# Gate weight sums and the split output weight of a Fourier layer formed during the attention layer and kept in DRAM

## The chip, the cores and the metric

The kernel runs on one core of one Trainium2 chip. A core has five engines that each work through a queue of their own: TensorE (PE) multiplies matrices, with weight loads (PEld) beside it; VectorE (DVE) and ScalarE (ACT) work on tiles; GpSimd (POOL) does both small vector work and DMA issues; SyncE (SP) issues DMAs. Engines wait for each other by semaphores. Data lies in DRAM, is loaded into SBUF by 16 DMA engines, and matmuls write to PSUM. The metric is the time of one execution in microseconds (us).

## The reference

Two layers work on a prompt of 2048 tokens and a sample of 512, each with 1024 channels, in float32: a banded attention with a gate, then Fourier mixing with a gate. A final norm follows.

```python
def attention_layer(x, g, w_in, w_out, sink, rel_bias):
    h = rmsnorm(x, g)
    z = h @ w_in
...
    o = banded_gqa_with_sink(q, k, v, rel_bias, sink)
    return x + (o * jax.nn.silu(gate)) @ w_out

def fourier_layer(x, g, w_gate, w_out):
    b, s, d = x.shape
    h = rmsnorm(x, g)
    hg = h.astype(jnp.float32).reshape(b, s, N_FGROUPS, FGROUP_CH)
    f = jnp.fft.fftn(hg, axes=(1, 3), norm="ortho").real
    f = f.reshape(b, s, d).astype(x.dtype)
    gate = h @ w_gate
    return x + (f * jax.nn.silu(gate)) @ w_out
```

`w_gate` and the Fourier layer's `w_out` (`w_fout` in the kernel) are 1024 x 1024.

## The kernel before

**Arithmetic.** A float32 value is held as two f32r tiles, a rounded high part and the remainder. `matmul3` (L81) makes one product out of three matmuls: high by high, high by low, low by high. So every weight has to be split before use: a cast makes the high part, a subtraction the low part.

**Attention phase** (`attention_phase`, from L116). The tokens go in five chunks of 512. In chunk 0 `load_w` (L87) loads each of 28 weights of 128 x 1024, casts it on ACT (L97), forms the remainder on POOL in four pieces of 128 x 256 (L102), and stores both parts to DRAM (`wsd`, 1 MB each); the later chunks load them from there. In each chunk a loop runs 64 steps, over 8 pairs of heads, four blocks of 128 queries and two heads, plus five steps in which the last ones drain. One step's `scores` is a pair of matmuls into the PSUM tile `spt` (L385), a DVE instruction that adds the bias and finds the extreme (L397, into `S`), an exponential on ACT (L401), a reciprocal (L404) and a scaling (L406) on DVE. Three steps later `transp` turns the scores on PE (L417) and splits them on ACT (L418) and DVE (L419) into `pts`; two steps after that `av` (L431) multiplies with the values; `out_evac` (L436 to L449) gates the result into the tiles `uT`, with two small instructions on POOL. Projections of the next heads, and at the end `out_proj` (L453), fill PE between the steps. SBUF tiles of the tag "x" (4 KB per partition: activations that are loaded and normed) come from a ring of four buffers, `S` from five, `spt` from two. A tile that takes a used buffer waits until the last reader of the old tile is done. The statistics of the next chunk run in the second half of a loop (i from 28 on), in tiles of tag "x".

**Seam and Fourier phase** (`fourier_phase`, from L561). Tiles come from two rings, `left` (24 buffers) and `right` (16). Token tiles are treated in ten pairs. The gate of a pair is a 2 x 2 block product done with seven products in place of eight (`gates`, L710): with w_gate cut into quarters B11, B12, B21, B22, the weights used are B11, T1 = B12 - B11, T2 = B22 - T1, B22, T3 = B22 - B12, N4 = B21 - B11 - T3, and B21, each in four row blocks of 128 x 512, each split. `build1` (L786) loads two pieces of w_gate (`w32g`), and makes the split parts of B11, T1, T2 and B22 in `left`, and those of B21, which POOL stores to `b21d`. `build2` (L801) loads the same pieces again (`w32h`) and makes T3 and N4 in `right`. The sums are DVE's, the casts ACT's (L586), the remainders DVE's or POOL's (L587). At the end of attention out_proj's last steps are interleaved with the four `build1` calls and with the norms of the first pair, whose `x1` loads go out on ACT's queue (L637); then the first pair's transposes (`turn`, L662), two `build2`, the transforms over channels (`z`), two `build2`, and the gates. In `gates` ACT copies each finished product out of PSUM (L746); in each pair B21 is loaded anew from `b21d` on SP's queue, two blocks ahead. After the last pair `load_res` (L590, called at L1007) loads w_fout in eight pieces of 512 KB and splits it on ACT (L600) and DVE (L601), before the output positions (`position`, `split_T` at L623, `finish`) use it as `wo`.

**Order.** Each engine executes its instructions in the order in which the program issues them. A DMA is issued from the queue of the engine named in the code, so SP, ACT and POOL can each hold DMAs back that stand behind a waiting instruction. In `inv_rms` a norm has one small POOL instruction (a power) between its sum and its scaling.

Of the kernel before, what the change touches and what calls it, by code (L numbers as in the profile page):

```python
# [31 lines left out]
LINE = 512  # L32
HALVES = ((1, 0), (1, 1), (0, 0), (0, 1))
# [5 lines left out]
def f32(ap):  # L39
    return ap.bitcast(F32)  # L40
# [3 lines left out]
def encoder(  # L44
# [25 lines left out]
    wsd = [dram.tile([P, 2, D], F32R, name=f"wsd{i}") for i in range(28)]  # L70

# [44 lines left out]
    def attention_phase():  # L116

        with ExitStack() as es:
# [365 lines left out]

            HB = [(b, j) for b in range(4) for j in range(2)]
# [7 lines left out]
            for c in range(len(CHUNKS)):  # L493
# [19 lines left out]
                for i in range(64 + LAG + AVLAG):  # L513
# [47 lines left out]
    def fourier_phase(tail):  # L561
        with ExitStack() as es:
# [26 lines left out]

            def load_res(w, name, stage):  # L590

                res, steps = [], []

                def load(half, k2):
                    w32 = stage(f"w32{name}{half}_{k2}")
                    SP.dma_start(w32, w[half, k2])
                    for kk in range(2):
                        t = left([P, 2, 512], F32R, f"wr{name}{half}_{k2}_{kk}")
                        src = w32[:, kk * 512 : kk * 512 + 512]
# [4 lines left out]
                for half in range(2):  # L604
                    for k2 in range(4):
                        steps.append(lambda half=half, k2=k2: load(half, k2))
                return res, steps
# [101 lines left out]

            def gates(pr, hooks):  # L710
# [5 lines left out]
                b21 = []  # L716

                def more():
                    if len(b21) < 4:
                        t = right([P, 2, 512], F32R, f"b21_{n}_{len(b21)}")  # L720
                        SP.dma_start(f32(t), f32(b21d[len(b21)]))
                        b21.append((t[:, 0], t[:, 1]))

                def x_step(k):
                    prod(X, A[0, 1], b21, (k,), True)
# [14 lines left out]
                more()  # L740
                more()
# [32 lines left out]
            b21d = [dram.tile([P, 2, 512], F32R, name=f"b21d{k}") for k in range(4)]  # L774
            wg = {w: [None] * 4 for w in ("B11", "T1", "T2", "B22", "T3", "N4")}

            def stage_w(w, k, name):

                rows = []
                for r in (k, k + 4):  # L780
                    t = left([P, 2, 512], F32, f"w32{name}{r}")
                    SP.dma_start(t, w[:, r // 2, :, (r % 2) * 512 : (r % 2) * 512 + 512].rearrange("h p c -> p h c"))
                    rows.append(t)
                return rows[0][:, 0], rows[0][:, 1], rows[1][:, 0], rows[1][:, 1]

            def build1(k):  # L786
                def w(name):
                    return left([P, 2, 512], F32R, f"w{name}_{k}")
# [390 lines left out]
```

## Time and profile before

| what | us |
|---|---|
| three timed runs | 1748.26, 1742.92, 1749.68 |
| median of them | 1748.26 |
| the profiled execution | 1746.94 |
| its span in the trace | 1745.2 |
| DVE busy in it | 1204.3 (69%) |
| ACT busy | 865.3 (50%) |
| POOL busy | 323.6 (19%) |
| chunk 1's 64 steps, first exponential to last | 286.5 to 431.5 |
| out_proj's last matmuls start | 1141.9 |

The span goes from the first to the last recorded instruction; 1.7 us of the execution lie around it. The mean granted clock of PE is 0.978. The trace shows for each instruction its start, its duration and, where its engine was idle, the event that ended the idle time. 342.6 MB are moved by DMA, at 196 GB/s in the mean.

### The profile page before, as it was taken

How to read it: one execution, taken by the hardware profiler on the slowest of the kernel's cores; microseconds unless marked ns; L12 is line 12 of the kernel's file. 1: busy time of each engine (PE TensorE's matmuls, PEld its weight loads, DVE VectorE, ACT ScalarE, POOL GpSimd, SP SyncE). 2: the span in 40 equal slices, each digit the busy share in tenths (PEclk: the TensorE clock that was granted, in tenths of full speed). 3: DMA queues.
4: the chain of work that ended last, by engine and by line, in shares of the span. 5: the costliest groups of instructions: out<-in, count | busy, mean ns of one | idle time of the engine just before them, and what ended most of it. 6: DMA issues, size and time to landing. Idle time of an engine off the chain costs nothing.

```text
span 1745.2 us, 25593 instructions
## 1 busy us (share of the span) xinstructions
PE 1663.0 (95%) x8980; PEld 1422.9 (82%) x8980; DVE 1204.3 (69%) x2826; ACT 865.3 (50%) x1966; POOL 323.6 (19%) x411
## 2 busy tenths in 40 slices
PE   9999899999999999899999999957999998999998
PEld 7877778888788888888888888846888886788886
DVE  5898655888448785288862888467667657888553
ACT  6677533675236663266641666335444545343221
POOL 2467630111301113011130111131000000111100
PEclk9999899999999999999999999978999999999999
DMA  8477775363663545744449443565565559763331
GB/s 304 170 284 300 263 289 194 132 213 136 220 236 134 184 152 184 265 139 166 161 151 325 139 139 128 190 238 193 187 223 187 195 175 336 283 223 118 139 106 49
DMA packets 95293, 342.59 MB, mean 196 GB/s; under 512 B 11019, under 2 KB 21259, under 8 KB 77244
## 3 DMA queue, kind: packets, MB, share of 16 engines
q1 hardware_dynamic: 87100, 298.74, 48.9%
q0 software_dynamic: 7632, 40.90, 6.0%
q8 instruction: 72, 1.18, 0.3%
q10 hardware_dynamic: 432, 1.31, 0.2%
q14 instruction: 57, 0.47, 0.1%
HBM read 267.47 MB, written 73.43 MB: 195 GB/s over the span
## 4 chain that ended last, share of the span: by engine, by line
PE 72%; DVE 12%; DMA 8%; issue 4%; ACT 3%; POOL 2%; SPq 1%; DVEq 0%; POOLq 0%; ACTq 0%
PE av L431 5%; PE spt L385 5%; PE pt L417 5%; PE qp L85 4%; PE qp L83 4%; PE qp L84 4%; PE gp L83 3%; PE gp L85 3%; PE gp L84 3%; PE op L83 3%; PE op L85 3%; PE op L84 3%; PE fo L85 3%; PE fo L83 3%; PE fo L84 3%
## 5 line engine op out<-in xcount | busy, mean ns | idle before, releaser
L401 ACT ACTIVATE S<-S 128x385 f32<-128x385 f32 (+1 forms) x320 | 191.1, 597 | 55.9 <-DVE S L397 54.9
L418 ACT CAST pts<-pt 128x384 fp32r<-128x384 f32 (+1 forms) x320 | 144.5, 454 | 116.2 <-PE pt L417 111.4
L419 DVE TENSOR_TENSOR pts<-pt,pts 128x384 fp32r<-128x384 f32 (+1 forms) x320 | 168.5, 526 | 42.7 <-ACT pts L418 40.1
L397 DVE CUSTOM_DVE_ANT_0 S<-spt,b 128x385 f32<-128x385 f32 (+1 forms) x320 | 168.8, 528 | 34.3 <-PE spt L385 29.5
L446 POOL TENSOR_TENSOR o<-o,s 128x256 f32<-128x256 f32 x75 | 55.3, 738 | 689.7 <-DVE o L442 678.2
L385 PE MATMUL spt<-kwin,qab 128*128 128x384 f32 (+1 forms) x640 | 159.1, 330 | 8.9 <-DVE S L397 8.9
L406 DVE TENSOR_SCALAR S<-S 128x384 f32<-128x384 f32 (+1 forms) x320 | 149.3, 467 | 9.1
L417 PE MATMUL pt<-ident,S 128*128 128x128 f32 x896 | 150.7, 274 | 1.0 <-DVE S L404 0.6
L385 PEld LDWEIGHTS spt<-kwin,qab 128*128 128x128 f32 x640 | 118.5, 189 | 38.0 <-DVE S L397 12.8
L83 PE MATMUL gp<-h,wg 128*128 128x512 f32 x320 | 137.7, 430 | 0.0
L83 PE MATMUL qp<-h,wq 128*128 128x512 f32 x320 | 137.1, 429 | 0.6 <-ACT wq L97 0.6
L431 PEld LDWEIGHTS av<-pts,v 128*128 128x128 f32 x896 | 126.6, 189 | 11.5 <-DVE pts L419 0.2
L431 PE MATMUL av<-pts,v 128*128 128x256 f32 x896 | 135.1, 284 | 0.0
L83 PE MATMUL op<-wo,uT 128*128 128x512 f32 x320 | 126.8, 399 | 2.9 <-DVE xr L476 2.9
L85 PE MATMUL fo<-wrf,tTu 128*128 128x512 f32 x320 | 126.2, 394 | 3.2 <-DVE tTu L623 3.2
L417 PEld LDWEIGHTS pt<-ident,S 128*128 128x128 f32 x896 | 114.0, 141 | 16.9 <-DVE pts L419 4.3
L83 PE MATMUL fo<-wrf,tTu 128*128 128x512 f32 x320 | 126.9, 396 | 0.0
L84 PE MATMUL op<-wo,uT 128*128 128x512 f32 x320 | 126.6, 396 | 0.0
L85 PE MATMUL qp<-h,wq 128*128 128x512 f32 x320 | 126.2, 394 | 0.1
L85 PE MATMUL gp<-h,wg 128*128 128x512 f32 x320 | 125.9, 393 | 0.0
L85 PE MATMUL op<-wo,uT 128*128 128x512 f32 x320 | 125.9, 395 | 0.0
L84 PE MATMUL fo<-wrf,tTu 128*128 128x512 f32 x320 | 125.8, 393 | 0.0
(322 smaller groups left out, 4052.8 us busy)
## 6 DMA issues: line engine op xcount, KB each, us to landing
wq<-wsd SPq DMA_DIRECT2D x32, 1024.0 KB, 4.9
wg<-wsd SPq DMA_DIRECT2D x32, 1024.0 KB, 6.6
wo<-wsd SPq DMA_DIRECT2D x32, 1024.0 KB, 4.9
b<-b21d SPq DMA_DIRECT2D x40, 512.0 KB, 5.1
x<-x1d SPq DMA_DIRECT2D x38, 512.0 KB, 4.4
b<-rowd SPq DMA_DIRECT2D x40, 384.0 KB, 4.2
xs<-in_x_dram SPq DMA_DIRECT2D x23, 512.0 KB, 7.3
xr<-in_x_dram SPq DMA_DIRECT2D x40, 256.0 KB, 5.1
```

Source lines behind the costliest of these rows:

```text
L83: PE.matmul(out, a[0], b[0], start=start, stop=False, skip_group_check=more)
L84: PE.matmul(out, a[0], b[1], start=False, stop=False, skip_group_check=more)
L85: PE.matmul(out, a[1], b[0], start=False, stop=stop, skip_group_check=more)
L385: PE.matmul(ps[:, 2 + k0 * P : 2 + k1 * P], q, kwin[g][:, part, b * P + k0 * P : b * P + k1 * P], start=part == 0, stop=part == 1,)
L397: DVE.tensor_tensor_reduce(out=s[:, e0:e1], in0=ps[:, 1 + e0 : 1 + e1], in1=st["bias"][:, j, 386 - e1 : 386 - e0][:, ::-1], scale=1.0, sca ...
L401: last_exp[0] = ACT.activation(s[:, e0:e1], s[:, e0:e1], AF.Exp, bias=mn, scale=-1.0, accum_out=den)
L406: DVE.tensor_scalar(s[:, ks], s[:, ks], den, None, ALU.mult)
L417: PE.transpose(ps[:, kb, :], s[:, 1 + kb * P : 1 + (kb + 1) * P], ident)
L418: ACT.copy(hi[:, k0:k1, j, :], ps[:, k0:k1, :])
L419: DVE.tensor_tensor(lo[:, k0:k1, j, :], ps[:, k0:k1, :], f32(hi[:, k0:k1, j, :]), ALU.subtract)
L431: PE.matmul(out, v, pt[:, kb].rearrange("p h q -> p (h q)"), start=kb == k0 and part == 0, stop=kb == k1 - 1 and part == 1,)
L446: eng.tensor_tensor(of, of, res["s"][:, cs], ALU.mult)
```

## The change

The sums and splits of w_gate, and the split of w_fout, are formed inside the loops of attention chunks 1, 2 and 3, one step of the list `EXTRA` per loop step i from 4 to 27, and stored to DRAM as pairs of f32r parts: `sumd` (28 tiles of 512 KB, B21 among them) and `foutd` (16 tiles). `keep` makes one of them in a tile of tag "x": the cast on ACT, the remainder on POOL in two pieces, the store from POOL's queue. The sums are POOL's in pieces too. In the Fourier phase the parts are loaded by POOL's queue: 16 tiles into `left` after the fifth step of out_proj's tail, 8 into `right` after the first pair's transposes, 16 of `wo` at the end. B21 is loaded by SP as before, but the list runs on over all pairs, so the blocks of the next pair are loaded while this one is computed. The first pair's norms are issued two steps earlier, in reversed order. w_gate is read once (8 loads on SP in the loops, 4.2 MB) instead of twice; 44 stores (23 MB) are added, and 40 loads on POOL's queue (21 MB) take the place of the 8 loads of w_fout and the 16 of w_gate in the Fourier phase.

```diff
+SUMS = ("B11", "T1", "T2", "B22", "T3", "N4", "B21")
...
+    evd = dram.tile([4, 2, P, D], F32, name="evd")
+    sumd = {w: [dram.tile([P, 2, 512], F32R, name=f"{w}d{k}") for k in range(4)] for w in SUMS}
+    foutd = [dram.tile([P, 2, 512], F32R, name=f"foutd{k}") for k in range(16)]
...
+            def pieces(out, a, b, op):
+
+                for i in range(2):
+                    cs = slice(i * 256, i * 256 + 256)
+                    POOL.tensor_tensor(out[:, cs], a[:, cs], b[:, cs], op)
+
+            def keep(dst, src):
+
+                t = ap.tile([P, 2, 512], F32R, tag="x", bufs=4, name="kept")
+                ACT.copy(t[:, 0], src)
+                pieces(t[:, 1], src, f32(t[:, 0]), ALU.subtract)
+                POOL.dma_start(f32(dst), f32(t))
+
+            def gate_sums(k):
+
+                q = {}
+
+                def load():
+                    for r, a, b in ((k, "B11", "B12"), (k + 4, "B21", "B22")):
+                        t = ap.tile([P, 2, 512], F32, tag="x", bufs=4, name=f"w32g{r}")
+                        src = w_gate[:, r // 2, :, (r % 2) * 512 : (r % 2) * 512 + 512]
+                        after(SP.dma_start(t, src.rearrange("h p c -> p h c")), last_exp[0])
+                        q[a], q[b] = t[:, 0], t[:, 1]
+
+                def kept(w, src):
+                    return lambda: keep(sumd[w][k], q[src])
+
+                def sums():
+                    pieces(q["B22"], q["B22"], q["B12"], ALU.subtract)
+                    pieces(q["B12"], q["B12"], q["B11"], ALU.subtract)
+
+                def more():
+                    pieces(q["B11"], q["B11"], q["B22"], ALU.add)
+                    pieces(q["B21"], q["B21"], q["B11"], ALU.subtract)
+
+                return [load, kept("B11", "B11"), kept("B22", "B22"), kept("B21", "B21"), sums, kept("T3", "B22"),
+                        kept("T1", "B12"), more, kept("T2", "B11"), kept("N4", "B21")]
+
+            def fout_parts(half, k2):
+                st = []
+
+                def load():
+                    st.append(ap.tile([P, 2, 512], F32, tag="x", bufs=4, name=f"w32f{half}_{k2}"))
+                    after(SP.dma_start(st[0].rearrange("p k c -> p (k c)"), w_fout[half, k2]), last_exp[0])
+
+                return [load] + [lambda kk=kk: keep(foutd[half * 8 + k2 * 2 + kk], st[0][:, kk]) for kk in range(2)]
+
+            EXTRA = {1: [gate_sums(0), gate_sums(1)], 2: [gate_sums(2), gate_sums(3)],
+                     3: [fout_parts(h, k2) for h in range(2) for k2 in range(4)]}
...
+                    if i == 3:
+                        extra = [s for steps in EXTRA.get(c, []) for s in steps]
+                    if 4 <= i < 28 and extra:
+                        extra.pop(0)()
...
-            def load_res(w, name, stage):
...
-                        ACT.copy(t[:, 0], src)
-                        DVE.tensor_tensor(t[:, 1], src, f32(t[:, 0]), ALU.subtract)
-                        res.append((t[:, 0], t[:, 1]))
...
+            b21 = []
+
+            def more():
+
+                k = len(b21)
+                if k < 4 * len(pairs):
+                    t = right([P, 2, 512], F32R, f"b21_{k}")
+                    SP.dma_start(f32(t), f32(sumd["B21"][k % 4]))
+                    b21.append((t[:, 0], t[:, 1]))
+
...
-                b21 = []
...
-                    prod(X, A[0, 1], b21, (k,), True)
+                    prod(X, A[0, 1], b21[4 * n : 4 * n + 4], (k,), True)
...
-            b21d = [dram.tile([P, 2, 512], F32R, name=f"b21d{k}") for k in range(4)]
...
-            def stage_w(w, k, name):
...
-            def build1(k):
...
-                b11, b12, b21, b22 = stage_w(w_gate, k, "g")
-                wg["B11"][k] = split(w("B11"), b11)
-                DVE.tensor_tensor(b12, b12, b11, ALU.subtract)
-                wg["T1"][k] = split(w("T1"), b12)
-                DVE.tensor_tensor(b11, b22, b12, ALU.subtract)
-                wg["T2"][k] = split(w("T2"), b11)
-                wg["B22"][k] = split(w("B22"), b22, POOL)
-                t = w("B21")
-                split(t, b21, POOL)
-                POOL.dma_start(f32(b21d[k]), f32(t))
...
-            def build2(k):
...
-                b11, b12, b21, b22 = stage_w(w_gate, k, "h")
-                DVE.tensor_tensor(b22, b22, b12, ALU.subtract)
-                DVE.tensor_tensor(b21, b21, b11, ALU.subtract)
-                DVE.tensor_tensor(b21, b21, b22, ALU.subtract)
-                wg["T3"][k] = split(w("T3"), b22)
-                wg["N4"][k] = split(w("N4"), b21, POOL)
+            def load_sums(place, *names):
+                for w in names:
+                    for k in range(4):
+                        t = place([P, 2, 512], F32R, f"w{w}_{k}")
+                        POOL.dma_start(f32(t), f32(sumd[w][k]))
+                        wg[w][k] = (t[:, 0], t[:, 1])
...
-            builds = [lambda k=k: build1(k) for k in range(4)]
             for i, s in enumerate(tail):
                 s()
-                if i in (4, 6):
-                    pairs[0].norms((i - 4) // 2, ACT)
-                if i % 2 and builds:
-                    builds.pop(0)()
+                if i in (2, 4):
+                    pairs[0].norms((4 - i) // 2, ACT)
+                if i == 5:
+                    load_sums(left, "B11", "T1", "T2", "B22")
...
-            build2(0)
-            build2(1)
+            load_sums(right, "T3", "N4")
+            more()
+            more()
             for i, hf in HALVES:
                 pr.z(i, hf)
-            build2(2)
-            build2(3)
...
-            wo, loads = load_res(w_fout, "f", x_tile)
-            for s in loads:
-                s()
+            wo = []
+            for k in range(16):
+                t = left([P, 2, 512], F32R, f"wo{k}")
+                POOL.dma_start(f32(t), f32(foutd[k]))
+                wo.append((t[:, 0], t[:, 1]))
```

More of the change, by code (lines that the diff above doesn't have):

```diff
@@ L588, in split @@
                 return t[:, 0], t[:, 1]
-            def load_res(w, name, stage):
[L592 to L599, printed above, removed]
-                        ACT.copy(t[:, 0], src)
-                        DVE.tensor_tensor(t[:, 1], src, f32(t[:, 0]), ALU.subtract)
-                        res.append((t[:, 0], t[:, 1]))
[L604 to L607, printed above, removed]
             def split_T(src, name, flip=False):
@@ L715, in gates @@
                 X = bank(f"X{n}")
-                b21 = []
[L718 to L722, printed above, removed]
                 def x_step(k):
-                    prod(X, A[0, 1], b21, (k,), True)
+                    prod(X, A[0, 1], b21[4 * n : 4 * n + 4], (k,), True)
                     more()
@@ L738, in hook @@
                         h()
-                more()
-                more()
                 four = range(4)
@@ L872, in combine @@
                     SP.dma_start(gsd[i] if gi == 0 else evd[gi - 1, i] if i < 2 else odd[gi - 1, i - 2], r[i])
-            evd = dram.tile([4, 2, P, D], F32, name="evd")
             pr = pairs[0]
```

10 lines of the change are left out of this document (removed).

## The prediction, made before the change was run

> **What bounds the kernel now.** The page's busy shares and slices come first, to find where TensorE (PE) isn't the bound.
>
> ```profile
> PE 1663.0 (95%) x8980; PEld 1422.9 (82%) x8980; DVE 1204.3 (69%) x2826; ACT 865.3 (50%) x1966; POOL 323.6 (19%) x411
> PE   9999899999999999899999999957999998999998
> POOL 2467630111301113011130111131000000111100
> PEclk9999899999999999999999999978999999999999
> ```
>
> PE works 95% of the span, so a gain can only lie where it rests: slices 26 and 27, about 1134 to 1222 us, the seam between the phases. POOL is nearly empty after chunk 0, the room that the change uses. Next the waits of PE (total, times, longest), and the seam's timeline (start, duration, operation, wait and releaser).
>
> ```profile
> PE trb L662 <- DVE x L639: 16.4, 2, 16.1
> PE W L83 <- ACT c L746: 16.3, 1, 16.3
> PE spt L385 <- DVE S L397: 8.9, 6, 2.8
> PE X L83 <- DMA b<-b21d: 5.7, 6, 2.2
> PE fo L85 <- DVE tTu L623: 3.2, 1, 3.2
> ...
> 1158.45 1.97 PE L662 MATMUL trb<-ident,x 128*128 128x128 f32 x8 [16.13 <-DVE x L639]
> ...
> 1190.50 0.79 PE L83 MATMUL W<-wT,S 128*128 128x512 f32 x1 [16.28 <-ACT c L746]
> ```
>
> The two longest waits are one cause. The first transpose waits for a norm whose x1 load stands on ACT's queue behind casts that wait for w_gate; the second waits for a copy (L746) that stands on ACT behind casts of the second read of w_gate. Last, the windows: start and end, length, busy us and count of PE, PEld, DVE, ACT, POOL, granted clock, DMA share, GB/s.
>
> ```profile
> 160.00:230.00 70.00, 60.51 (x293) 49.19 (x292) 52.02 (x121) 37.02 (x84) 46.49 (x64) 0.90 0.76 265
> 300.00:360.00 60.00, 60.00 (x347) 52.55 (x346) 51.60 (x162) 40.42 (x103) 8.87 (x12) 1.00 0.42 141
> 1100.00:1150.00 50.00, 42.32 (x204) 34.70 (x202) 21.22 (x43) 14.30 (x31) 10.72 (x12) 0.96 0.69 249
> 1150.00:1180.00 30.00, 15.34 (x88) 13.37 (x88) 21.32 (x33) 12.88 (x23) 8.82 (x8) 0.73 0.55 188
> 1180.00:1200.00 20.00, 9.19 (x42) 7.51 (x42) 15.26 (x21) 12.33 (x24) 5.34 (x6) 0.66 0.69 244
> ...
> 1460.00:1470.00 10.00, 5.31 (x24) 4.14 (x25) 10.00 (x16) 6.20 (x12) 0.53 (x1) 0.83 0.88 319
> ```
>
> At the seam PE is half idle and its granted clock falls to 0.73 and 0.66. In chunk 1 (300 to 360) PE is full while DVE is already at 51.6 of 60; in chunk 0, where POOL splits weights (46.5 of 70), PE loses. The change moves chunk 0's kind of work into chunks 1 to 3.
>
> **Part 1, the seam: a gain.** Out_proj's last matmuls start at 1142, and the first pair's gates end at about 1211: 69 us. The work between, at full clock: four turns 4.0 us, 96 matmuls of 128x256 at their pitch of 0.12 us (11.5), 84 of 128x512 at 0.227 (19.1), together 34.6. So 34.4 us are lost: the two waits, the rest through the low clock. Removed are 16 loads of w_gate, 28 casts at 0.615, the DVE differences and splits, and four b21d stores. With no cast ahead of them the two x1 loads go out when ACT has made the last uT, 1120, and both norms are done by about 1130, ahead of out_proj's end: the first wait goes whole.
>
> What is late next are the 24 loads of sums, all on POOL's queue, in the order B11, T1, T2, B22, then T3, N4 once out_proj's weight buffers are free (1133 to 1142). Behind the first two stands the norm's small POOL instruction (pow), which waits for x1, so the stream runs from about 1130. At the 319 GB/s that 1460 to 1470 shows, four loads (2.1 MB) take 6.6 us, with SP's other reads about 7.5: T1 is in at 1138, T2 1145, B22 1153, T3 1160, N4 1168. PE wants them at about 1156, 1159, 1162, 1164 and 1177. Behind the last of them on POOL stand the pows of the second pair's norms; N4's last issue, eight loads ahead of its landing, comes at about 1155, and that pair's transposes are wanted at 1166, so they hide, with 11 us of cover. I leave 4 us (2 to 12) for the ramp: -30 (-22 to -33).
>
> **Part 2, B21.** Its reads now run ahead across pairs, where each pair began anew with two: of 5.7 us of X waits I take -3 (0 to -6).
>
> **Part 3, fout.** Eight SP loads, 16 ACT casts at 0.618 and 16 DVE subtractions at 0.684 become 16 POOL loads; that takes at most the 3.2 us wait and the slow clock around it. But bytes double, 4.2 to 8.4 MB, where the queue is full (1460 to 1480 moves 319 to 374 GB/s at shares of 0.88 and 1.02): 4.2 MB at 350 GB/s is 12 us of DMA time. The sample's table loads stand behind them on POOL. +2 (-8 to +8).
>
> **Part 4, attention: the loss.** Added are 44 keeps (28 for the gate, 16 for fout), each a cast on ACT, two pieces on POOL, and a 512 KB store that POOL issues, and 32 pieces for the sums. The rows of the same instructions (count: min/median/max):
>
> ```profile
> L102 POOL TENSOR_TENSOR wg<-w32g,wg x28: 712/737/783, 36.9 to 163.7; 128x256 fp32r<-128x256 f32 x28
> ...
> L586 ACT CAST wB<-w32g x12: 601/615/623, 1129.4 to 1161.3; 128x512 fp32r<-128x512 f32 x12
> ...
> L799 POOL DMA_DIRECT2D b21d<-wB x4: 571/582/597, 1136.2 to 1164.7; - x4
> ...
> DMA to landing us min/median/max: 4.3/5.2/7.2
> ```
>
> POOL gets 120 x 0.737 + 44 x 0.58 = 114 us, and ACT 44 x 0.615 = 27 us, over three chunks of some 150 us loops: room in the mean. The wait is the price. The "x" ring has four buffers, two held by the weights read, so the kept tile n needs the store of n-2 landed, and ACT, which runs in order, stands at that cast with all later exponentials (L401) and pts copies (L418) behind it; PE waits for those. One keep costs 0.615 + 1.474 + 0.58 = 2.67 us plus the landing L, and two run at a time: 13 x (2.67 + L) / 2 from first to last keep of a chunk. That is 45, 51 and 64 us for L = 4.3, 5.2 and 7.2. ACT's order allots 17 exponentials in chunk 1 and 16 in chunk 2 between these; at 2.30 us a step (64 from 286.5 to 431.5) 39 and 37 us. A tile is used some 4 us after it is ready (L397 of one step ends at 320.85, its bank is wanted again at 324.56), which absorbs 4. At L = 5.2: 51 - 39 - 4 = 8 in chunk 1, 10 in chunk 2, 1 in chunk 3, where three buffers serve the stores: +19. At 4.3 it is 6, at 7.2 about 48; the b21d row was measured in windows of 188 to 249 GB/s, the loop moves 141 plus what is added, so I take its median.
>
> Two queues more are passed. On SP the 16 loads (16 x 512 KB) wait for a ring buffer, and behind them stand the projections' weights (wq, wg); I count nothing, as the "w" ring holds four, about half a group of eight steps, 9 us; without that cover SP adds up to the same lag again, which is C's size. On POOL, out_evac's two small instructions wait behind the pieces; their product uT is wanted only by out_proj at the loop's end, so that hides too.
>
> DVE's scale (L406) also suffers beside POOL: 0.405 us mean in 300 to 360, 0.606 in 100 to 160, 0.852 in 160 to 230. A step has 2.30 x 8.4 / 60 = 0.32 us of DVE to spare, so +0.2 hides; +0.45 would cost 0.13 x some 60 steps, 8 us, at the same steps that the store wait delays, so I don't add it. [...]
>
> **Sum.** The profiled run took 1746.94 (span 1745.2, 1.7 around it): 1746.9 - 30 - 3 + 2 + 19 = 1735; the median of the three runs is 1.3 above it, so 1736.
>
> **Rivals.**
> A, the forecast: 1736, by itself 1726 to 1748. For it: waits of 16 us with a named cause; a ring too short by arithmetic.
> B, the stores keep pace: L near 4.3, as the loop's DMA share of 0.42 suggests; attention costs 6: 1723. Against it: chunk 0, where no ring of two holds ACT, lost 8.9 in spt waits alone. [...]
> C, the other side: landing grows as POOL, reads of the loop and stores meet. L = 7.2 costs 48: 1736 + 29 = 1765, slower. It decides from where the attention cost passes 31 us (L about 6.1). For it: wsd<-wg stores of 1 MB land in 9.2 us in chunk 0; against: that stretch moves 298 GB/s, the loop half.
> D, POOL's stream is late at the seam: at the 249 GB/s of 1100 to 1150, 20 loads and 5 MB of SP's reads, 15.5 MB, take 62 us from 1130, N4 in at 1192 against 1177: 15 lost, gain 15: 1751, no change. For it: one queue, with pow in front; against: 319 to 374 GB/s seen later.
>
> **How the numbers follow.** Chances: A 0.47, B 0.18, C 0.23, D 0.12. A measurement of this kernel tells about 0.5%, 8.7 us, from no change: faster is under 1739.5, slower over 1757. A is faster in 0.36 and the same in 0.11; B faster 0.18; C slower 0.21, same 0.02; D same 0.09, slower 0.03. So 0.54, 0.22, 0.24. The range goes from 1714 (B with the seam's -33 and B21's -6) to C's 1766. A's own range stands above.
>
> **What would show it.** Right: the trb and W waits gone, clock 0.95 or more from 1140 to 1200; spt, pt and av waits of about 19 us in chunks 1 and 2 while i is 4 to 28, behind an ACT that waits for kept stores; L406 at 0.5 to 0.6 there. Wrong: a seam still over 50 us; a W or Z wait for DMA (D); waits in the loops over 40 us (C) or under 8 (B); fo waits over 10 us at 1440 to 1480.

## The result, and the profile after

Over twelve runs each the changed kernel takes 1753.14 us (1748.47 to 1757.76), the kernel before 1748.12; the ratio is 1.0033, with an interval of 1.0021 to 1.0046. The change costs about a third of a per cent, where the forecast had a gain of 12 us. The profiled run took 1751.27 us, 4.3 more than the one before (1746.94).

First the busy slices and the waits of PE in the profile after (total us, times, longest).

```profile
PE   9999899899989899999999999998999998999998
POOL 2467732721305511305313011121000001112000
PEclk9999999899999999999999999998999999999999
```

```profile
PE spt L389 <- DVE S L401: 31.5, 20, 3.5
PE As L87 <- ACT gs L931: 7.7, 1, 7.7
PE z L87 <- DVE xr L480: 7.6, 1, 7.6
```

The hole of slices 26 and 27 (counted from 0) is gone, with both waits of 16 us. In its place PE has lost a tenth in slices 7 and 13, in the loops of chunks 1 and 2, with POOL at 7 and at 5 there; slice 11, where POOL is at 0, is the gap between these loops. The spt waits went from 8.9 to 31.5 us. The windows show the two sides, chunk 1's loop and the seam (columns as before).

```profile
300.00:360.00 60.00, 50.60 (x264) 42.65 (x264) 46.12 (x113) 33.66 (x85) 41.35 (x61) 0.91 0.67 229
...
1183.00:1225.00 42.00, 34.39 (x193) 30.57 (x192) 21.98 (x35) 19.30 (x36) 6.22 (x12) 0.88 0.89 349
```

From 300 to 360, where PE was full, it now works 50.6 of 60 us and its granted clock is 0.91; DVE and ACT do less there than before (46.1 against 51.6, 33.7 against 40.4), so neither of them is the bound: they stand. Over the steps 4 to 28 of the three loops:

```profile
293.08:365.42 72.34, 62.94 (x334) 53.38 (x334) 56.85 (x147) 41.64 (x105) 46.59 (x68) 0.93 0.67 237
535.19:608.13 72.94, 63.91 (x338) 53.24 (x337) 61.65 (x148) 42.56 (x106) 46.66 (x68) 0.95 0.63 228
780.59:848.33 67.74, 62.32 (x349) 52.42 (x348) 52.44 (x148) 43.65 (x109) 38.68 (x57) 1.00 0.81 287
```

Before, the same steps took 55.5, 57.5 and 57.5 us, with PE busy throughout. They now take 42.5 us more: PE stands idle in 23.9 of these, and the other 18.6 lie in matmuls that take longer.

Where the time went is read by setting the same events of the two traces beside each other: the last exponential of attention, out_proj's last matmul, the last matmul of the first and of the tenth pair's last gate product (W from N4), and the last matmul of the output (fo).

| stretch, us | before | after | difference | forecast |
|---|---|---|---|---|
| start to attention's last exponential | 1104.2 | 1144.9 | +40.7 | +19 |
| to out_proj's last matmul | 37.8 | 37.8 | 0 | 0 |
| the seam, to the first pair's last gate matmul | 68.7 | 42.0 | -26.7 | -30 |
| to the last pair's last gate matmul | 242.5 | 246.9 | +4.4 | -3 (B21) and, with the next row, |
| to the last output matmul | 283.9 | 270.1 | -13.8 | +2 (fout) |

The sum of the differences is 4.6 us. The last two stretches exchange some 30 matmuls at their border (1372 in the last one before, 1339 after), so their sum, -9.4 against a forecast of -1, says more than each of them. By chunk, the first exponentials of chunks 2, 3 and 4 come 17.6, 30.7 and 40.7 us later. Nearly all of it falls on the steps up to i = 24: in chunk 1 the shift is +3.7 at step 8, +8.6 at 16, +16.8 at 24, and then stands.

### The profile page after: what moved, and what is told of

It reads as the page before. It is cut to its first block, busy times and chain, and to the rows that moved or that the text cites. A ratio compares the mean times of both kernels' runs of the same rounds, so it can differ in the third digit from the quotient of the medians.

```text
span 1749.5 us, 25848 instructions
## 1 busy us (share of the span) xinstructions
PE 1667.1 (95%) x8980; PEld 1422.5 (81%) x8980; DVE 1190.6 (68%) x2774; ACT 857.7 (49%) x1966; POOL 440.9 (25%) x599
## 5 line engine op out<-in xcount | busy, mean ns | idle before, releaser
L389 PE MATMUL spt<-kwin,qab 128*128 128x384 f32 (+1 forms) x640 | 162.5, 336 | 31.7 <-DVE S L401 31.5
L410 DVE TENSOR_SCALAR S<-S 128x384 f32<-128x384 f32 (+1 forms) x320 | 174.1, 544 | 8.9
L450 POOL TENSOR_TENSOR o<-o,s 128x256 f32<-128x256 f32 x75 | 55.2, 736 | 416.1 <-DVE o L446 409.7
L87 PE MATMUL gp<-h,wg 128*128 128x512 f32 x320 | 139.2, 435 | 0.0
L87 PE MATMUL qp<-h,wq 128*128 128x512 f32 x320 | 137.3, 429 | 0.6 <-ACT wq L101 0.6
L89 PE MATMUL gp<-h,wg 128*128 128x512 f32 x320 | 127.1, 397 | 0.0
L87 PE MATMUL fo<-wo,tTu 128*128 128x512 f32 x320 | 125.9, 393 | 1.2 <-DVE x L973 1.2
L88 PE MATMUL gp<-h,wg 128*128 128x512 f32 x320 | 126.8, 396 | 0.0
L89 PE MATMUL qp<-h,wq 128*128 128x512 f32 x320 | 126.2, 394 | 0.1
L88 PE MATMUL qp<-h,wq 128*128 128x512 f32 x320 | 125.6, 393 | 0.0
```

The source lines that it names most:

```text
L87: PE.matmul(out, a[0], b[0], start=start, stop=False, skip_group_check=more)
L88: PE.matmul(out, a[0], b[1], start=False, stop=False, skip_group_check=more)
L89: PE.matmul(out, a[1], b[0], start=False, stop=stop, skip_group_check=more)
L389: PE.matmul(ps[:, 2 + k0 * P : 2 + k1 * P], q, kwin[g][:, part, b * P + k0 * P : b * P + k1 * P], start=part == 0, stop=part == 1,)
L410: DVE.tensor_scalar(s[:, ks], s[:, ks], den, None, ALU.mult)
L450: eng.tensor_tensor(of, of, res["s"][:, cs], ALU.mult)
```

## The experiments

In what follows "attention's end" is the shift of the last exponential against the kernel before, from the traces; a ratio is of times to the kernel before, with its interval. Of the names in the expectations, "lock" is the rival that POOL's instructions hold DVE: in the kernel before the scale (L406) took up to 3.421 us in 50 to 231, where POOL is busy for 111.2 of 181 us, and up to 0.839 in 231 to 1110, where it is busy for 136.0 of 879. "Work" is the rival that what was added to ACT and POOL is in the way as such.

### What holds the loops: stores, ACT, POOL alone

**No stores.** One line of `keep` is left out, and the Fourier phase loads other DRAM of the same size.

```diff
-                POOL.dma_start(f32(dst), f32(t))
```

> The changed kernel without the 44 stores of kept tiles; the Fourier phase loads as many bytes from wsd in their place, so its weights are not those of the reference. In the changed kernel's trace the last exponential of attention lies 40.8 us later than before (1144.9 against 1104.2). Theory (ring): ACT stands at the cast of a kept tile until a store two tiles back has landed; without stores nothing of that is left, and attention's end moves by 3 to 12 us in place of 41; time 1715 to 1727. [...]

Measured: 1743.79 us, ratio 0.9989 (0.9975 to 1.0003); attention's end +28.7. Without stores 12 of the 41 us go, and 28.7 stay: the theory of the forecast, that the ring alone holds ACT, falls. By chunk, the loops lose 13.4, 12.9 and 2.0 us in place of 16.6, 14.0 and 10.0. The waits that the theory is about do stand in the changed kernel, for instance in 285 to 365 (waits of ACT, all that name a kept tile's store or POOL):

```profile
ACT kept L498 <- DMA B11d<-kept: 6.9, 2, 4.7
ACT uT L452 <- POOL o L450: 6.0, 5, 1.6
ACT kept L498 <- DMA B22d<-kept: 2.3, 1, 2.3
ACT kept L498 <- DMA B21d<-kept: 2.3, 2, 1.9
ACT kept L498 <- POOL kept L493: 1.7, 1, 1.7
```

ACT's waits for POOL at uT were 4.5 us in this window before, so in the changed kernel the stores are the longer hold there. Without stores the waits for POOL take their place:

```profile
ACT uT L452 <- POOL o L450: 10.4, 6, 4.2
ACT kept L498 <- POOL kept L493: 4.8, 2, 3.5
ACT kept L498 <- POOL w32g L493: 3.8, 3, 1.6
```

In chunk 1 of this run no scale of DVE took over 0.9 us, so the scale's holds, which come up below, have no part in its 13.4 us.

In chunk 3 of the changed kernel the hold has one more link: the loads of w_fout, on SP's queue, wait for a store to free their buffer, and ACT waits for the loads (waits of SP in 770 to 850, of ACT in 780 to 850):

```profile
SPq L532 <- DMA foutd<-kept: 21.1, 4, 10.3
ACT kept L498 <- DMA w32f<-in_w_fout_dram: 10.0, 4, 3.7
```

**Casts on POOL.**

```diff
-                ACT.copy(t[:, 0], src)
+                for i in range(2):
+                    cs = slice(i * 256, i * 256 + 256)
+                    POOL.tensor_copy(t[:, 0, cs], src[:, cs])
```

> The changed kernel with the cast of a kept tile made by POOL in two pieces of 128x256 in place of ACT: ring, stores and POOL's other work stay, but the wait for a store now holds POOL, not ACT. Theory (ring): exponentials are free again, attention's end moves by 5 to 15 us in place of 41; time 1717 to 1730. Rival (lock): POOL does more, not less, so DVE is held more: attention's end moves by 41 to 55; time 1753 to 1768. Rival (ACT's work): 27 us of casts are gone from ACT: 15 to 25 in place of 41; time 1730 to 1738, and no store wait seen in the chain.

Measured: 1754.68 us, 1.0049 (1.0033 to 1.0065); attention's end +43.6. ACT has no kept cast left, and yet it stands, now at another place (waits of ACT, 285 to 365):

```profile
ACT uT L452 <- POOL o L450: 20.2, 5, 9.4
```

Out_evac multiplies on POOL (L450), and ACT casts the product into uT (L452). With POOL's queue full of pieces that product comes late, and ACT, in order, waits with all later exponentials behind it: 20.2 us in five times, against 4.5 in six before.

**POOL's pieces alone, in pairs.** Two pieces per step on a scratch tile, in the kernel before.

```diff
+                    if 1 <= c < 4 and 4 <= i < (26 if c < 3 else 20):
+                        for _ in range(2):
+                            after(POOL.tensor_tensor(scr, scr, scr, ALU.mult), last_exp[0])
```

> The kernel before with 120 pieces of 128x256 on POOL added in the loops of chunks 1 to 3 (two per step, on a scratch tile, nothing waits for them): no casts, no stores, no loads, the seam as before. Theory (ring): such work alone costs little, attention's end moves by 0 to 6 us; time 1748 to 1755. Rival (lock): most of the 41 us appear here: attention's end moves by 25 or more; time 1773 to 1790.

Measured: 1754.24 us, 1.0037 (1.0014 to 1.0061); attention's end +6.8.

**The same in runs of eight**, at two places in the four-step rhythm of out_evac (the diff shows the first; the second has `i % 4 == 3`).

```diff
+                    if 1 <= c < 4 and i % 4 == 1 and 4 <= i < (28 if c < 3 else 20):
+                        for _ in range(4 if i > 24 else 8):
+                            after(POOL.tensor_tensor(scr, scr, scr, ALU.mult), last_exp[0])
```

> The kernel before with the same 120 pieces on POOL as in the run with pieces alone, but in runs of eight in a row (5.9 us) in each fourth loop step, at i mod 4 = 1, where out_evac's own two POOL instructions have just been issued and the next come three steps (6.9 us) later. In pairs they moved attention's end by 6.8 us. Theory (backlog: POOL's queue holds ACT at the cast of uT and of kept tiles): nothing of out_evac stands behind a run, so 5 to 12 us; time 1749 to 1757. Rival (lock for a whole run): DVE's scale (L406) is held up to 5.9 us by each of 16 runs, 2 or more beyond the slack: 25 to 45; time 1772 to 1790.

> The same runs of eight, one step ahead of out_evac (i mod 4 = 3), so that its product on POOL (L446) stands behind a run, and ACT's cast of uT (L448) waits for it with all later exponentials behind it. Theory (backlog): ACT is held 2 to 5 us by each of 16 runs; attention's end moves by 15 to 40 us more than with the runs at i mod 4 = 1, and the waits of ACT's L448 for POOL are 30 us or more longer than before. Rival (lock): the place of a run does not matter, the same time as there within 5 us.

Measured: 1753.10 us, 1.0032 (1.0015 to 1.0049) and 1757.20 us, 1.0056 (1.0035 to 1.0078); attention's end +7.3 and +10.8.

**Runs with two inputs, and built as in `keep`.** The first reads two halves of another tile; the second subtracts an f32r part from float32 into f32r, and only the first piece of a run is ordered. The diff is that of the second, against the runs of eight.

```diff
-                            after(POOL.tensor_tensor(scr, scr, scr, ALU.mult), last_exp[0])
+                            ins = POOL.tensor_tensor(w3[:, 1, cs], w2[:, cs], f32(w3[:, 0, cs]), ALU.subtract)
+                            if j == 0:
+                                after(ins, last_exp[0])
```

> As the runs of eight at i mod 4 = 1, but each piece reads two different halves of a tile of tag x and writes a third place, as the pieces of keep do (the earlier ones read and wrote one place only, and DVE's scale was never held longer than 0.9 us by them; in the changed kernel L410 was held up to 3.65 us, until POOL's run of pieces ended). Theory (lock for a whole run, when POOL reads two places): L406 is held 3 us or more, often, and attention's end moves by 15 to 40 us; time 1762 to 1787. Rival (no such lock; L410's long times are something else): as before, 6 to 9 us; time 1751 to 1757.

> Runs of eight pieces at i mod 4 = 1 as before, but built as in keep: float32 minus the high part, f32r out, two halves in turn, and only the first piece of a run ordered behind an exponential, so that the others are ready at once. Theory (POOL's runs hold DVE when each next piece stands ready): L406 held 2 us or more several times a chunk, attention's end moves by 12 to 35 us; time 1758 to 1782. Rival (what holds DVE in the changed kernel is not the pieces as such): max under 1 us as in the other runs, 4 to 9 us; time 1750 to 1757.

Measured: 1752.23 us, 1.0041 (1.0023 to 1.0058), attention's end +5.6; and 1747.90 us, 1.0010 (0.9997 to 1.0024), +0.6. In all five DVE's scale took at most 1.0 us in chunks 1 to 3. But the traces limit what they say. `after` orders instructions where the program is built and makes nothing wait on the chip, so part of the pieces ran ahead of the loop (of chunk 1's 44 pieces 12 in pairs, 30 in the last), and a run came behind out_evac's instructions at both places: the waits of ACT for POOL at uT were 7.2 us in both, in 285 to 365. What is shown is that POOL's work that holds nobody up costs 1 to 11 us; a backlog ahead of out_evac, which one of them was to make, was not made by it.

### Two holds side by side

**ACT free of POOL.** To the casts on POOL comes uT's, in chunks 1 to 3.

```diff
-                    ACT.copy(uT[:, 0, cs], of)
+                    if eng is POOL and c in (1, 2, 3):
+                        POOL.tensor_copy(uT[:, 0, cs], of)
+                    else:
+                        ACT.copy(uT[:, 0, cs], of)
```

> The changed kernel with the cast of kept tiles on POOL, and in chunks 1 to 3 also out_evac's cast of uT on POOL: ACT has no instruction left in the loops that waits for POOL or for a store. With the kept casts alone on POOL attention's end still moved by 43.7 us, with 20 us of waits of ACT for POOL at uT's cast in chunk 1's first 80 us. Theory (backlog): attention's end moves by 8 to 20 us; time 1720 to 1735. Rival (lock): POOL has more work still and DVE is held as before: 35 to 50; time 1747 to 1762.

Measured: 1743.22 us, 0.9967 (0.9946 to 0.9988); attention's end +31.4. Better by 12 than the casts alone, but far from free. What holds now is DVE: its scale takes 45.8 us in chunk 1's 64 steps, where it took 26.0 before, with single ones of 3.2 to 3.9. The changed kernel has the same at fewer places: 36.5 us there, with three over 1 us in place of nine. Its timeline (start, duration, operation), first DVE, then POOL in the same 4 us:

```profile
309.46 3.65 DVE L410 TENSOR_SCALAR S<-S 128x256 f32<-128x256 f32 x1
```

```profile
308.79 1.45 POOL L493 TENSOR_TENSOR w32g<-w32g,w32g 128x256 f32<-128x256 f32 x2
310.19 0.73 POOL L450 TENSOR_TENSOR o<-o,s 128x256 f32<-128x256 f32 x1
310.88 1.39 POOL L493 TENSOR_TENSOR kept<-w32g,kept 128x256 fp32r<-128x256 f32 x2
312.25 0.71 POOL L453 TENSOR_TENSOR uT<-o,uT 128x256 fp32r<-128x256 f32 x1
312.91 0.59 POOL L500 DMA_DIRECT2D T1d<-kept  x1
```

An instruction of 0.36 us takes 3.65: it begins inside a row of six POOL instructions without a gap, and ends at the end of that row, where POOL comes to issue a DMA.

**The scale in another form.** It writes a sum too, which nothing reads, and takes longer (medians of 0.614 us, and 0.423 in the changed kernel, where the scale is L410).

```diff
-                    DVE.tensor_scalar(s[:, ks], s[:, ks], den, None, ALU.mult)
+                    DVE.tensor_scalar(s[:, ks], s[:, ks], den, None, ALU.mult, ALU.add, accum_out=mn)
```

> [...] Rival (only backlog and stores): L410's longer time adds to a full DVE, attention's end moves by 41 or more; time 1753 to 1770.

> The kernel before with DVE's scale in the form that also writes a sum, and nothing else: the price of that form. In the changed kernel chunk 4, where nothing is added, lost 4 us by it. Expected by all theories: 4 to 7 us in each of chunks 1 to 4 and 0 to -3 in chunk 0, attention's end moved by 12 to 25 us; time 1758 to 1772.

Measured: 1774.04 us, 1.0162 (1.0132 to 1.0193) with the change, 1771.27 us, 1.0142 (1.0123 to 1.0162) on the kernel before; attention's end +65.5 and +25.1. In the changed kernel L410 reads (min/median/max ns):

```profile
L410 DVE TENSOR_SCALAR_CACHE_REDUCE S<-S x320: 459/614/618, 54.2 to 1170.5; 128x384 f32<-128x384 f32 x128, 128x256 f32<-128x256 f32 x32
```

No instance is over 0.618 us, in chunk 0 either: the hold belongs to the old form (up to 3.421 us there before) and to POOL, and it is gone. But the change still costs 40.4 us on top of this form's own price (65.5 - 25.1), as much as without it (40.7). The longest took 3.655 us in the one form and 0.618 in the other; why the two differ no run shows. Removing that hold alone gave nothing; ACT still stood at its kept casts for 15.0 us in 285 to 365 (13.2 in the changed kernel).

**Both away**: ACT free of POOL, and the scale in the other form.

> The changed kernel with both: ACT free of POOL and of stores in the loops (casts of kept tiles and of uT on POOL), and DVE's scale in the form that was not held by POOL (it writes an unused sum too). Each alone left 31 and 65 us. Theory (two holds side by side, each enough by itself: ACT behind stores and POOL, DVE behind POOL's runs): with both gone attention's end lies only 0 to 12 us behind the kernel before with the same form of the scale, which runs beside it. Rival (a third cause: DMA traffic, or PE's own): still 25 us or more behind that kernel.

Measured: 1747.91 us, 1.0006 (0.9993 to 1.0019); attention's end +39.6, that is 14.5 behind the same form on the kernel before, just over the theory's 12. Up to step 24 of chunk 1 it loses 2.2 us where that form on the kernel before loses 1.6, and the changed kernel 17.5. What is left comes at once between steps 24 and 32 of each of chunks 1 to 3, and the waits of DVE in 285 to 365 name it:

```profile
DVE s L346 <- POOL o L450: 10.2, 2, 7.9
```

DVE writes the next gate tile s into a buffer whose reader, out_evac's product on POOL, is 7.9 us late. A third engine's queue is held by the same backlog; POOL has the casts on top in this kernel, and in the changed kernel no such wait shows in that window. So the holds stand side by side: taking one away shows the next, and their costs do not add. In chunk 1, up to step 24, DMA traffic and work as such cost no more than these 2.2 us.

### Placing the work elsewhere

**Spread** over four chunks, one step in two, and **placed** away from out_evac:

```diff
+            fsteps = [s for h in range(2) for k2 in range(4) for s in fout_parts(h, k2)]
+            EXTRA = {c: {4 + 2 * j: s for j, s in enumerate(gate_sums(c - 1))} for c in range(1, 5)}
+            EXTRA[4].update({26 + 3 * j // 2: s for j, s in enumerate(fsteps)})
```

> The changed kernel with the same steps spread: one set of gate sums in each of chunks 1 to 4, one step in every second loop step (i 4 to 22), and the parts of w_fout in chunk 4 at two of three steps from i 26 to 60. Theory (ring): a keep then has 4.6 us or more of loop per step, 9.2 for two, against the 2.67 us plus a landing of 3 to 5.6 that it needs, so ACT hardly waits: attention's end moves by 3 to 12 us; time 1715 to 1727, 1 to 2% faster than before. Rivals (lock, work): the work is the same, only elsewhere: attention's end still moves by 30 to 41; time 1742 to 1755.

```diff
+                return {
+                    5: load, 9: kept("B11", "B11"), 10: kept("B22", "B22"), 13: kept("B21", "B21"),
+                    14: diff("B22", "B22", "B12", sub), 17: kept("T3", "B22"), 18: diff("B12", "B12", "B11", sub),
+                    19: diff("B11", "B11", "B22", add), 21: kept("T1", "B12"), 22: diff("B21", "B21", "B11", sub),
+                    25: kept("T2", "B11"), 26: kept("N4", "B21"),
+                }
...
+            EXTRA[4].update(zip([i for i in range(28, 64) if i % 4 != 0][:24], fsteps))
```

> One gate set in each of chunks 1 to 4 from i 5 to 26, each sum a step of its own, keeps mostly at i mod 4 = 1 and 2, so that out_evac's POOL instructions (i mod 4 = 0) do not stand behind them, and w_fout's parts in chunk 4 from i 29 to 62, never at i mod 4 = 0. The plain spreading moved attention's end by 30 us, 8, 6, 5 and 10 in chunks 1 to 4. Theory (holds by POOL's runs and by stores): less of each, 2 to 5 us a chunk, 10 to 20 in all; time 1722 to 1734. Rival (the work as such): 25 to 32 as with plain spreading; time 1738 to 1745.

Measured: 1742.62 us, 0.9975 (0.9962 to 0.9989), attention's end +29.8; and 1754.43 us, 1.0045 (1.0033 to 1.0058), +44.4. Both were to be spread and were not: in the traces a gate set's seven casts stand behind exponentials 5, 6, 7, 8, 10, 11 and 11 of chunk 1 in the first, 7 to 13 in the second, one per step and no thinner than the first set's in the changed kernel (5 to 11). The order along an engine is made when the program is built, and a place in the source did not bind it. What was tested is only one gate set per chunk in place of two, with w_fout's parts late in chunk 4 (behind exponentials 27 to 60 and 31 to 59).

**Between the loops.** The steps are interleaved with out_proj's tail, the key and value projections and the first query projection (`ex()` takes one from the list); two gate sets ahead of chunk 2, two ahead of 3, w_fout's parts ahead of 4.

```diff
                     s()
+                    ex()
```

> The changed kernel with all its extra steps taken out of the loops of 64 steps and put between them, beside the dense projections: two gate sets ahead of chunk 2 and two ahead of chunk 3, the parts of w_fout ahead of chunk 4, one step after each group of out_proj's tail, of the key and value projections and of the first query projection. There PE has 70 us of its own work and waits for ACT and DVE only at the ends. Theories backlog and lock agree: no step-by-step chain to be held, attention's end moves by 0 to 12 us; time 1712 to 1727. Rival (work or DMA as such, wherever it is): 25 to 41; time 1738 to 1753.

Measured: 1780.47 us, 1.0176 (1.0149 to 1.0204); attention's end +73.1, a miss. ACT waits 33 us for the stores of kept tiles in the first gap, where its casts for keys and values stand behind it. Then the same with nothing on ACT or SP:

```diff
-                ACT.copy(t[:, 0], src)
+                for i in range(2):
+                    cs = slice(i * 256, i * 256 + 256)
+                    POOL.tensor_copy(t[:, 0, cs], src[:, cs])
...
-                        after(SP.dma_start(t, src.rearrange("h p c -> p h c")), last_exp[0])
+                        after(POOL.dma_start(t, src.rearrange("h p c -> p h c")), last_exp[0])
```

> As the kernel with all steps in the gaps between the loops, but nothing of them is on ACT or SP: the casts are POOL's pieces and the loads of w_gate and w_fout go out on POOL's queue. That kernel lost 20, 20 and 32 us in the three gaps, with ACT standing 29 us in the first of them at casts that waited for stores, ahead of the casts of the key projections. Theory (ACT held by stores): attention's end moves by 0 to 12 us in place of 73; time 1712 to 1727, faster than both kernels. Rival (DMA or POOL in the gaps is in the way as such, by late weights): 30 or more; time 1740 or more.

Measured: 1760.49 us, 1.0083 (1.0058 to 1.0109); attention's end +49.8, of which 31 come in one step of chunk 4. In fences, the wait of PE, the wait of ACT, POOL's timeline there, and the waits of POOL in 930 to 1034:

```profile
1032.40 1.01 PE L397 MATMUL spt<-kwin,qab 128*128 128x384 f32 x2 [29.01 <-DVE S L409]
```

```profile
ACT uT L460 <- POOL o L458: 32.5, 1, 32.5
```

```profile
1028.84 0.58 POOL L510 DMA_DIRECT2D foutd<-kept  x1 [0.30 <-POOL kept L501]
1029.44 0.73 POOL L458 TENSOR_TENSOR o<-o,s 128x256 f32<-128x256 f32 x1
```

```profile
POOL kept L508 <- DMA w32f<-in_w_fout_dram: 49.0, 8, 8.3
```

POOL is not done with w_fout's parts until 1029.4 and only then makes out_evac's first product of the chunk; ACT stands 32.5 us for it at uT, and PE 29.0. POOL is late because it stands itself, for loads of w_fout that its own queue issues. No store and no held scale is in this chain: a short POOL instruction stands behind other work in POOL's queue, and ACT's queue stands for it.

**Only the gate's part**, the changed kernel with w_fout as before:

```diff
-                     3: [fout_parts(h, k2) for h in range(2) for k2 in range(4)]}
...
+            wo, loads = load_res(w_fout, "f", x_tile)
+            for s in loads:
+                s()
```

> The changed kernel with the part of w_fout undone: chunk 3 has no extra steps, and w_fout is loaded and split after the last gates as before. My forecast's term for fout at its place was +2 us, with 1 us in chunk 3: time 3 us less than the changed kernel, 1747 to 1753. Rival (from the traces: chunk 3's loop lost 9 us and the stretch after the last gates won about 8): the same time within 3 us, attention's end moved by 31 in place of 41, and the matmuls of the last stage late by the 8 us again.

Measured: 1744.27 us, 0.9994 (0.9983 to 1.0005); attention's end +28.6, the tenth pair's end 237.1 us behind the first's, the output's end 278.8 behind that. By the two ratios that is some 7 us less than the changed kernel, more than the 3 of the forecast's term, where the rival had the same time; attention's end and the later last stage are near the rival's.

**One set in each gap, all on POOL**, and w_fout's parts late in chunk 4's loop, or as before.

```diff
+            EXTRA = {c: [gate_sums(c - 1)] for c in range(1, 5)}
+            fsteps = [s for h in range(2) for k2 in range(4) for s in fout_parts(h, k2)]
+            LAST = {26 + 3 * j // 2: s for j, s in enumerate(fsteps)}
```

> One gate set in each gap ahead of chunks 1 to 4, beside the dense projections, wholly on POOL (its loads, casts, pieces and stores), and w_fout's parts in chunk 4's loop from i 26 to 60 as in the plain spreading, with their casts on ACT. With two sets in a gap on POOL the gaps ahead of chunks 2 and 3 lost 6 and 2 us and the loops behind them 3 and 5, where POOL was not done in time; w_fout's parts from i 26 on lost 3 in the plain spreading; and with w_fout's parts in the gap ahead of chunk 4 PE waited 29 us once, as ACT's cast of uT stood for a product on POOL behind them. Theory (ACT and DVE are held wherever POOL is behind in a loop): attention's end moves by 5 to 17 us; time 1716 to 1731, the fastest of all. Rival (late weights through more DMA in the gaps, ACT's make_h held): 25 us or more; time 1738 or more.

> The same, with w_fout loaded and split after the last gates as before. In the changed kernel undoing w_fout's part took 12 us off the loops and gave 3 us back behind the gates. Expected: attention's end 3 to 4 us less late than with w_fout's parts in chunk 4, the stretch behind it 0 to 8 us longer: the same time as that run within 5 us. If the parts loaded by POOL's queue win nothing at their place, it is the faster of the two.

Measured: 1734.46 us, 0.9936 (0.9923 to 0.9950), and 1728.51 us, 0.9897 (0.9881 to 0.9912): both beat both kernels, the second by a per cent. Attention's end is +18.1 and +20.1, over the range stated, but from the first step to the last of each loop of the second the shift grows by 0.6 us at most, and falls by 1.1 in chunk 2: the loops cost nothing any more. All of it lies in the gaps, 6 to 7 us in three of them and 2 in the fourth. The second was expected to have attention's end 3 to 4 us earlier than the first and a longer stretch behind it; it has 2.0 later, and the stretch is 4.5 shorter. Its windows of chunk 1's loop and of the gap behind it:

```profile
300.00:360.00 60.00, 60.00 (x346) 52.47 (x345) 51.64 (x159) 39.34 (x100) 8.12 (x11) 1.00 0.44 152
440.00:515.00 75.00, 67.31 (x365) 59.21 (x364) 28.19 (x52) 18.02 (x42) 39.99 (x55) 0.95 0.81 295
```

In the gap DMA is at 0.81 and 295 GB/s (0.69 and 242 before), and PE waits 3.1 us for the last evacuation of out_proj and 2.3 for a key's evacuation on ACT (0.8 before); a wait of 2.2 for late weights stood there before too (2.3). Whether fewer bytes there would win the rest was not tried.

## Why the prediction was wrong

**What bounds the kernel, and part 1, the seam:** right in mechanism and size. Both waits went, and 26.7 us of the 30 came, within its bounds. What is late next was not the weights: the last load of out_proj's residual (xr) went out on SP only at 1187.75 and landed 6.8 us later, and `z` waited 7.6 us for the bank that it frees. The granted clock from 1183 to 1225 is 0.88, under the 0.95 that the forecast named as a sign. Neither the late weights of D nor its price showed.

**Part 2, B21:** -3 forecast; with the gate's part alone the ten pairs take 237.1 us in place of 242.5, -5.4, within the bounds. The X waits of 5.7 us are gone there.

**Part 3, fout:** +2 forecast at its place. Against the gate's part alone, the stretch to the last gates is 9.8 us longer, with a wait of 7.7 for ACT, which stands for a load on SP's queue (`gl` from `gsd`, transforms stored before) that lands among the sixteen, and the stretch behind 8.7 shorter: +1.1. But its price in chunk 3's loop, for which I had 1, is 10 (the shift grows from 30.7 to 40.7; without this part it stays at 28.7), so the part as a whole loses.

**Part 4, attention:** here it failed, 40.7 for 19. PE's idle time in the loops came close to what was summed, 9.4, 9.0 and 5.4 us in chunks 1, 2 and 3 against 8, 10 and 1. But the sum had no term for work that slows beside such waits, and that is 18.6 us. By the granted clock of 0.93 and 0.95, the 55.5 and 57.5 us of work in chunks 1 and 2 would grow by 7 us, which is an estimate; the rest of the 18.6 stays open.

The path was wrong too, for the waits were laid to the stores alone. The step that failed is the sentence "On POOL, out_evac's two small instructions wait behind the pieces; their product uT is wanted only by out_proj at the loop's end, so that hides too". The product is wanted at once by ACT's cast of uT, which is next in ACT's queue, and the buffers that it reads are wanted by DVE (the gate tile s). The profile before already had the row, over the whole run:

```profile
ACT uT L448 <- POOL o L446: 56.2, 56, 1.8
```

I asked who needs the data, not which queue stands for it. In the changed kernel itself the stores' hold covers this one (6.0 us at uT in 285 to 365, 4.5 before); with the stores gone 28.7 of the 40.7 us stay, and ACT stands 19.0 us for POOL in 285 to 365. With more work on POOL such waits grew to 20.2, 32.5 and 10.2 us in three other kernels.

The second failure is "so I don't add it", of DVE's held scale. It did not add, as the run without it shows (40.4 with it removed), but with ACT freed 31.4 us stayed, and only with both away 14.5. I counted one hold, and the ones behind it were left out. The third is in chunk 3, "where three buffers serve the stores" and "I count nothing" of SP's loads: these waited 21.1 us for stores and ACT 10.0 for the loads. What the stores cost by themselves no run tells; taking them away gave 3, 1 and 8 us by chunk, against 8, 10 and 1 forecast, with landings of 2.9 to 5.6 us (medians of the eight kinds).

**The sum and the rivals:** with 41 in place of 19 the sum gives 1757, within 6 us of the profiled run; the rest is the seam, 3 short, and the stretches behind it, 8 better than forecast. That the time lies next to D's 1751 is chance: D had half the seam's gain lost, and the seam gave 26.7. C named the right place, ACT at the loops, with the wrong reason: its median landing of 7.2 us was not reached, though single stores took up to 9.2. Two ends of the range are slips that change nothing: B with the better seam and B21 is 1717, not 1714, and C's 1765 became 1766.

## What to carry to other kernels

For work moved onto an idle engine, list every instruction already on that engine, and for each the next instruction in any other queue that waits for it or for its buffers: here that queue, ACT's with single waits of up to 32.5 us, set the slack, not the consumer of the data. The holds here stood at the same steps, did not add and did not show one by one (40.4 us stayed without DVE's, 31.4 with ACT freed, 14.5 with both away): take such holds away together, or move the work to a place where no short chain runs through the engine, as between the loops, where the shift within a loop grew by 0.6 us at most (gate sets alone, all on POOL). And read in the trace whether work that was placed in the source stands there: here it did not, in seven kernels.

## What the runs showed of the hardware that was not expected

A DVE tensor_scalar from SBUF to SBUF (0.36 us) was held for 3.65 us by a row of POOL instructions, not by one of 0.73; in the form that writes a sum the longest in two kernels were 0.618 and 0.620. The DMA issue behind the row is not needed: in the run without stores one was held 3.71 us, to the end of a row with no DMA issue behind it. Yet in the four kernels with rows of four to eight pieces on POOL it took no more than 1.0 us in chunks 1 to 3. A row without gaps is not enough: in the changed kernel twelve scales that began in such a row took over 1.0 us, and 24 that began with over 1 us of it to go did not. What makes a row hold for its whole length stays open.
